# A bidirectional hybrid encoder layer: two small SBUF tiles that shift every pool's address, three score buffers in the attention, its output bank copied out at once, and a new order table

## The chip, the cores and the metric

One core of one Trainium2 chip runs the kernel. The metric is the device time in microseconds, as the median of several runs. The trace of one execution is read beside it.

## The reference, cut to what matters

The layer is FFN1, then a mixing stage of attention and RWKV-7 side by side, then FFN2; 1024 tokens, model width 1024, FFN width 2816, all in float32.

```
x = x + 0.5 * post1(FFN1(pre1(x)))          # SwiGLU: (silu(h @ w_gate) * (h @ w_up)) @ w_down
z = pre2(x) @ w_in                          # attention q|k|v and RWKV r|k|v|low-rank columns
attention: 8 heads of 64, rotary, three banded patterns (128,1), (512,4), (2048,16),
           mixed by their softmax denominators
RWKV-7:    8 heads, forward and backward delta-rule scans over the tokens, summed
x = x + post2(concat(attention, rwkv) @ w_out)
x = x + 0.5 * post3(FFN2(pre3(x)))
```

## The kernel before, in words

Large products are made from a rounded high part and a remainder: each operand is split into two `float32r` tiles, high (h) and low (l), and a product is three matmuls, h·h, h·l and l·h, of 128 rows by 128 stationary columns by up to 512 moving columns. The FFNs save one product in eight by Strassen's scheme, so a weight block meets seven sums of activation blocks (`_GateUp.multiply`, `down`). FFN1 takes the trace's first 620 us, FFN2 everything from about 1570 us on. Small products (scores of the far pattern, values, scan) are plain float32.

The attention works head by head. `far` handles the pattern of dilation 16, `near` the other two together, in eight query tiles t. For each t, `scores` makes up to 640 scores in PSUM, adds the bias and takes the minimum on DVE into the SBUF tile `sb`, and ACT takes the exponential there; `turn` transposes `sb` on PE and copies it to `e12`; `values` multiplies `e12` with v into the PSUM tile `po`, the one buffer of tag "o". When the last t is through, `near` weighs `po` by `c12` into the SBUF tile `ya`. `attention` loads the v tile of the far pattern, `v3`, into one buffer. The pool of all these tiles, `attw`, has two buffers for a tag that names no number.

Nothing is issued in the order in which it is written. `_Tape` records every operation with its tile accesses. `order` ranks them by a table of costs, going forward and backward over the graph, then adds to the rank of the operations with recorded numbers a to b what `LEADS` says, for one engine or all, and sweeps once more. The result is one fixed order per engine, which `play` issues. A buffer more or less, or another row of `LEADS`, can therefore move instructions anywhere between the FFNs.

SBUF is laid out by two stacks of pools. The left stack begins at byte 4224 of each partition with `cons` (the constants), and the right stack hangs from byte 229344 downwards. A tile takes its size rounded up to 32 bytes. `cons` holds, among others, two columns `eps0` and `eps1` and the column `root`, one float each and so 32 bytes each; `root` is written once by ACT and read by nobody.

Of the kernel before, what the change touches and what calls it, by code (L numbers as in the profile page):

```python
# [11 lines left out]
F32 = mybir.dt.float32  # L12
F32R = mybir.dt.float32r
AF = mybir.ActivationFunctionType
OP = mybir.AluOpType
# [5 lines left out]
NK, NT, NJ = D // 128, S // 128, DFF // 128  # L21
# [11 lines left out]
def _ap(src, off, pat):  # L33
    return bass.AP(tensor=src.tensor, offset=src.offset + off, ap=pat)


LEADS = (
# [6 lines left out]
)  # L44
LOADS = {AF.Exp: 1, AF.Sqrt: 2, AF.Silu: 3, AF.Tanh: 4}

# [682 lines left out]
class _Kernel:  # L729
# [537 lines left out]
    def near(self, psum, p, h, q1, q2, k, v, far, between):  # L1267

        nc, V, A, G, T = self.nc, self.nc.vector, self.nc.scalar, self.nc.gpsimd, self.nc.tensor
        hs = slice(h % 2 * 64, h % 2 * 64 + 64)  # L1270
        m, d, M, c12, c3 = (p.tile([128, NT], F32, name=n, tag=n) for n in ("m", "dn", "M", "c12", "c3"))
        po = psum.tile([128, NT, 64], F32, name="po", tag="o")
        S_, E_ = {}, {}
        keys = lambda t: (max(0, t - 2), min(NT, t + 3))

        def scores(t):
            k0, k1 = keys(t)
            n, qs = (k1 - k0) * 128, slice(t * 128, (t + 1) * 128)
            bias = self.bias12[:, (k0 - t + 2) * 128:(k0 - t + 2) * 128 + n]
            s = S_[t] = p.tile([128, 640], F32, name="sb", tag="sb")  # L1280
            for c in range(0, n, 512):
                e = min(n, c + 512)
                ps = psum.tile([128, 512], F32, name="s12", tag="w")
                T.matmul(ps[:, :e - c], q1[:, qs], k[:, k0 * 128 + c:k0 * 128 + e], start=True, stop=False)
                T.matmul(ps[:, :e - c], q2[:, qs], k[:, k0 * 128 + c:k0 * 128 + e], start=False, stop=True)
                V.tensor_tensor_reduce(out=s[:, c:e], in0=ps[:, :e - c], in1=bias[:, c:e], scale=1.0,
                                       scalar=m[:, t:t + 1] if c else 3e38, op0=OP.add, op1=OP.min,
                                       accum_out=m[:, t:t + 1])
            A.activation(s[:, :n], s[:, :n], AF.Exp, scale=-1.0, bias=m[:, t:t + 1], accum_out=d[:, t:t + 1])

        def turn(t):
            n, s = (keys(t)[1] - keys(t)[0]) * 128, S_.pop(t)
            et = E_[t] = p.tile([128, 640], F32, name="e12", tag="e12")
            for c in range(0, n, 512):
                w = min(n - c, 512)
                pt = psum.tile([128, 512], F32, name="pt12", tag="w")
                for i in range(w // 128):
                    T.transpose(pt[:, i * 128:(i + 1) * 128], s[:, c + i * 128:c + (i + 1) * 128], self.ident)
                A.copy(et[:, c:c + w], pt[:, :w])

        def values(t):
            (k0, k1), et = keys(t), E_.pop(t)
            for i in range(k1 - k0):
                for c in range(0, 128, 64):
                    T.matmul(po[c:c + 64, t, :], et[:, i * 128 + c:i * 128 + c + 64], v[:, k0 + i, hs], start=(i == 0),
                             stop=(i == k1 - k0 - 1))

        for step in range(NT + 2):
            if step < NT:
                between(step)  # L1310
                scores(step)
            if 1 <= step < NT + 1:
                turn(step - 1)
            if step >= 2:
                values(step - 2)
        f = far
        fm, fd = f[:, :, 64], f[:, :, 65]
        V.tensor_tensor(M, m, fm, op=OP.min)
        V.tensor_tensor(c12, m, M, op=OP.subtract)
        V.tensor_tensor(c3, fm, M, op=OP.subtract)  # L1320
        A.activation(c12, c12, AF.Exp, scale=-1.0)
        A.activation(c3, c3, AF.Exp, scale=-1.0)
        V.tensor_tensor(d, d, c12, op=OP.mult)
        V.tensor_tensor(M, fd, c3, op=OP.mult)
        V.tensor_tensor(d, d, M, op=OP.add)
        V.reciprocal(d, d)
        V.tensor_tensor(c12, c12, d, op=OP.mult)
        V.tensor_tensor(c3, c3, d, op=OP.mult)
        y = p.tile([128, NT, 64], F32, name="ya", tag="sb3", bufs=1)
        V.tensor_tensor(y, po, c12[:, :, None].to_broadcast([128, NT, 64]), op=OP.mult)  # L1330
        f3 = f[:, :, 0:64]
        G.tensor_tensor(f3, f3, c3[:, :, None].to_broadcast([128, NT, 64]), op=OP.mult)
        G.tensor_tensor(y, y, f3, op=OP.add)
        G.tensor_tensor(f3, y, y, op=OP.mult)
        V.tensor_reduce(out=self.ss_a[:, :, h], in_=f3, op=OP.add, axis=AX.X)
        self.nc.scalar.dma_start(_ap(self.ya_d, h * 64, [[512, 128], [128 * 512, NT], [1, 64]]), y)

    def attention(self, psum, p):
        X, F, ST = {}, {}, {}

        def load(pr):
            v3 = p.tile([128, 8, 128], F32, name="v3", tag="v3", bufs=1)
            for j in range(2):
                self.load(v3[j * 64:j * 64 + 64],
                          _ap(self.v_att, j * 512 + pr * 128, [[16 * 512, 64], [2 * 512, 8], [1, 128]]))
            vn = p.tile([128, NT, 128], F32, name="vn", tag="vn")
            self.load(vn, _ap(self.v_att, pr * 128, [[512, 128], [128 * 512, NT], [1, 128]]))
            q, k = (p.tile([128, S], F32, name=n, tag=n) for n in ("qp", "kp"))
            self.load(q, self.q_d[pr])
            self.load(k, self.kt_d[pr])  # L1350
            X[pr] = q, k, v3, vn

        def far(h):
            q, k, v3, _ = X[h // 2]
            for r in self.far(psum, p, h, q, k, v3):
                F[h] = r
                yield

        def stack(h):
            ST[h] = self.stacked(p, h)  # L1360

        load(0)
        for _ in far(0):
            pass
        stack(0)
        for h in range(H):
            nxt = far(h + 1) if h + 1 < H else iter(())

            def between(t):
                if t == 0 and h % 2 and h + 1 < H:  # L1370
                    load((h + 1) // 2)
                if t in (1, 3, 5):
                    next(nxt, None)
                if t == 4 and h + 1 < H:
                    stack(h + 1)

            self.near(psum, p, h, *ST.pop(h), X[h // 2][3], F.pop(h), between)
# [319 lines left out]
    def constants(self):  # L1697
        nc, io = self.nc, self.io
# [1 line left out]
        self.ident = cons.tile([128, 128], F32, name="ident")  # L1700
        make_identity(self.tc.nc, self.ident)
        self.g2c = self.column("mix_pre_g", NK)
        self.eps = {c: cons.tile([128, 1], F32, name=f"eps{i}") for i, c in enumerate((1.0, 0.5))}
        for c, t in self.eps.items():
            nc.vector.memset(t, EPS / (c * c))
        nc.scalar.activation(cons.tile([128, 1], F32, name="root"), self.eps[1.0], AF.Sqrt)
        self.gneps = cons.tile([128, 1], F32, name="gneps")
        nc.vector.memset(self.gneps, GN_EPS)
        self.h1_d, self.h2_d = self.dram("h1", [S, D]), self.dram("h2", [S, D])
# [53 lines left out]
    def run(self):  # L1763
        nc = self.nc
# [3 lines left out]
        natural = list(range(NT))  # L1768
        with self.top as top:

            self.constants()
            s_xn = ExitStack()
            xp = self.pool(s_xn, "xn")
# [3 lines left out]
            with ExitStack() as st:  # L1777
# [6 lines left out]
                f = self.factors(x, xt)  # L1784
# [31 lines left out]
                p = self.pool(s_f1, "ffn1")  # L1816
# [18 lines left out]
                y = [self.finish_low(rows, psum, ct, [ps[ct, half] for half in range(2)]) for ct in LO]  # L1835
# [4 lines left out]
                po = _Banks(w=pw, o=self.pool(s_ps, "ps_o", 1, space=PSUM))  # L1840
# [69 lines left out]
            for j in range(2):  # L1910
                for n in (1, 2):
                    gate_up.ready[n, j] = self.halves(wf, self.slab(wf, gate_up.source(j, 0, n - 1), bufs=2, queue=nc.gpsimd),
                                                      bufs=4)
            gb, late = self.row_bcast(hand, "mix_post_g"), {}
            f = self.factors(f0, None)
# [37 lines left out]
            with ExitStack() as st:  # L1953
# [13 lines left out]
                p, hand = self.pool(st, "ffn2", **R), self.pool(st, "hand3", **R)  # L1967
# [59 lines left out]
```

## Time and profile before

| | |
|---|---|
| median of 3 runs | 2223.08 us (2217.14 to 2230.62) |
| the profiled execution | 2219.22 us, of which the span from first to last instruction is 2217.4 us |
| busy: PE / DVE / ACT / POOL | 97% / 67% / 48% / 30% of the span |
| mean granted TensorE clock | 0.987 |
| matmul records | 14788 |

The span says how long the core worked; the profiled execution's own time has 1.8 us more around it. A busy engine is one that has an instruction in flight. Matmuls overlap: a 512-column matmul is in flight for about 395 ns, but the next one starts some 230 ns after it, so their rate is read from the starts, not from durations. [...]

### The profile page before, as it was taken

To read this page: it belongs to the slowest core of one execution; us is meant where nothing else is said; L and a number is where in the kernel's file an instruction comes from. 1 tells how busy PE (TensorE), PEld (TensorE's weight loads), DVE (VectorE), ACT (ScalarE), POOL (GpSimd) and SP (SyncE) were. 2 spreads that over 40 slices of the span, in tenths; PEclk is the share of its full clock that TensorE was granted. 3 is DMA by queue.
4 is the path that set the end of the run, shared out by engine and by line. 5 is a ranking of instruction groups with operands and counts; after the bars stand their busy time and mean duration, and the time that the engine had idled before them with its cause. 6 is when DMAs were issued, how large, how long until landed. Compare 5 with 4: busy or idle time off the path is not lost. (4 is left out here: it accounts for less than half of the span.)

```text
span 2217.4 us, 39926 instructions
## 1 busy us (share of the span) xinstructions
PE 2146.9 (97%) x14788; PEld 1738.5 (78%) x14788; DVE 1486.1 (67%) x2573; ACT 1064.0 (48%) x2026; POOL 662.4 (30%) x962
## 2 busy tenths in 40 slices
PE   6999999999999999999899998999899999999998
PEld 5888888878887888789687776767688888888887
DVE  8877767675575664663565557569976676776557
ACT  6333323354476655573666666456433323235453
POOL 3353444520000001142475661321053534451000
PEclk9999999999999999999899998999999999999999
DMA  5455444576463338776977757596254544458555
GB/s 152 133 166 162 158 161 138 180 272 213 152 233 121 122 135 278 209 233 205 264 219 194 178 138 179 128 283 204 85 182 139 176 141 149 138 198 308 187 179 185
DMA packets 364021, 403.36 MB, mean 182 GB/s; under 512 B 74418, under 2 KB 272306, under 8 KB 362804
## 3 DMA queue, kind: packets, MB, share of 16 engines
q1 hardware_dynamic: 319360, 309.47, 46.2%
q0 software_dynamic: 26416, 82.90, 11.0%
q10 hardware_dynamic: 18052, 8.46, 1.5%
q8 instruction: 116, 1.90, 0.4%
q14 instruction: 77, 0.63, 0.1%
HBM read 266.45 MB, written 134.28 MB: 181 GB/s over the span
## 5 line engine op out<-in xcount | busy, mean ns | idle before, releaser
L584 ACT ACTIVATE wh<-raw 128x512 fp32r<-128x512 f32 x264 | 163.7, 629 | 377.8 <-PE gu L584 304.4
L584 DVE TENSOR_TENSOR row<-gu,row 128x512 f32<-128x512 f32 x308 | 205.7, 686 | 193.3 <-PE gu L584 178.7
L584 POOL TENSOR_TENSOR row<-row 128x512 f32<-128x512 f32 x88 | 122.6, 1395 | 466.0 <-DVE row L584 448.5
L584 PE MATMUL gu<-xh,wh 128*128 128x512 f32 x704 | 253.9, 397 | 1.9 <-ACT row L584 1.6
L584 PE MATMUL gu<-xl,wh 128*128 128x512 f32 x704 | 253.6, 395 | 0.0
L584 PE MATMUL gu<-xh,wl 128*128 128x512 f32 x704 | 251.9, 395 | 0.0
L584 DVE TENSOR_TENSOR wl<-raw,wh 128x512 fp32r<-128x512 f32 x264 | 209.6, 813 | 18.1 <-ACT wh L584 14.4
L584 DVE TENSOR_TENSOR gwl<-graw,gwh 128x512 fp32r<-128x512 f32 (+2 forms) x187 | 115.8, 624 | 116.0 <-PE pd L584 85.5
L584 PE MATMUL pd<-gh,gwh 128*128 128x512 f32 x616 | 176.7, 395 | 0.4 <-ACT gh L584 0.4
L584 PE MATMUL pd<-gl,gwh 128*128 128x512 f32 x616 | 176.5, 395 | 0.0
L584 PE MATMUL pd<-gh,gwl 128*128 128x512 f32 x616 | 176.3, 395 | 0.0
L584 ACT ACTIVATE gwh<-graw 128x512 fp32r<-128x512 f32 (+2 forms) x187 | 102.8, 554 | 152.9 <-PE pd L584 119.2
L584 PEld LDWEIGHTS gu<-xh,wh 128*128 128x128 f32 x704 | 132.4, 189 | 33.0 <-ACT row L584 1.8
L584 PEld LDWEIGHTS gu<-xl,wh 128*128 128x128 f32 x704 | 132.2, 188 | 30.0
L584 PEld LDWEIGHTS gu<-xh,wl 128*128 128x128 f32 x704 | 131.9, 188 | 30.2
L584 PEld LDWEIGHTS pd<-gh,gwh 128*128 128x128 f32 x616 | 115.4, 188 | 27.5 <-ACT gh L584 0.8
L584 PEld LDWEIGHTS pd<-gh,gwl 128*128 128x128 f32 x616 | 115.5, 188 | 26.9
L584 PEld LDWEIGHTS pd<-gl,gwh 128*128 128x128 f32 x616 | 115.4, 188 | 27.0 <-DVE gl L584 0.5
L584 ACT ACTIVATE gh<-raw 128x512 fp32r<-128x512 f32 x160 | 99.4, 630 | 53.2 <-PE pd L584 31.0
L584 DVE TENSOR_TENSOR gl<-raw,gh 128x512 fp32r<-128x512 f32 x160 | 109.0, 694 | 20.7 <-ACT gh L584 20.7
L584 POOL TENSOR_TENSOR ws<-ws 128x512 f32<-128x512 f32 x88 | 118.0, 1340 | 2.9
L584 PE MATMUL zr<-xh,zh 128*128 128x512 f32 x320 | 107.0, 400 | 5.7 <-ACT zh L584 4.2
(298 smaller groups left out, 4817.6 us busy)
## 6 DMA issues: line engine op xcount, KB each, us to landing
d_hid<-row POOLq DMA_DIRECT2D x154, 256.0 KB, 3.0
graw<-d_hid SPq DMA_DIRECT2D x132, 256.0 KB, 3.0
raw<-in_ffn_w_up_dram SPq DMA_DIRECT2D x88, 256.0 KB, 3.2
ws<-in_ffn_w_down_dram SPq DMA_DIRECT2D x88, 256.0 KB, 4.3
d_ws<-ws POOLq DMA_DIRECT2D x88, 256.0 KB, 2.8
raw<-d_ws SPq DMA_DIRECT2D x88, 256.0 KB, 3.3
raw<-in_ffn_w_gate_dram SPq DMA_DIRECT2D x84, 256.0 KB, 3.2
raw<-in_ffn_w_down_dram SPq DMA_DIRECT2D x66, 256.0 KB, 3.3
```

The costliest lines, as they stand in the source:

```text
L584: i = getattr(getattr(self.nc, op.eng), op.method)(*op.args, **op.kwargs).ins
```

## The change

1. The column `root` moves into a second element of `eps0`, so `cons` is 32 bytes smaller and every pool of the left stack starts 32 bytes lower.
2. A tile `edge` of 120 floats (480 bytes) is put at the top of the right stack. Nothing reads or writes it; every pool of the right stack starts 480 bytes lower.
3. In `near`, `sb` and `e12` get three buffers; in `attention`, `v3` gets the pool's two.
4. `near` copies the PSUM tile `po` to `ya` on ACT, and DVE weighs `ya` in place; `ya` has a tag of its own and no longer shares the buffer of the far scores `sb3`.
5. The table `LEADS` has other rows. The costs and rules of the planner are as before.

```
-    (0, 1183, 8420, 0), (836, 1177, -1851), (1111, 1720, 1216), (2164, 2186, -51421, 1), (2215, 2730, 3599, 1),
...
+    (1213, 1316, 5853), (1562, 1602, 20982, 0), (1609, 1771, -10608, 0), (3774, 3934, 19691), (4092, 4123, 669, 0),
...
-            s = S_[t] = p.tile([128, 640], F32, name="sb", tag="sb")
+            s = S_[t] = p.tile([128, 640], F32, name="sb", tag="sb", bufs=3)
...
-            et = E_[t] = p.tile([128, 640], F32, name="e12", tag="e12")
+            et = E_[t] = p.tile([128, 640], F32, name="e12", tag="e12", bufs=3)
...
-        y = p.tile([128, NT, 64], F32, name="ya", tag="sb3", bufs=1)
-        V.tensor_tensor(y, po, c12[:, :, None].to_broadcast([128, NT, 64]), op=OP.mult)
+        y = p.tile([128, NT, 64], F32, name="ya", tag="ya", bufs=1)
+        A.copy(y, po)
+        V.tensor_tensor(y, y, c12[:, :, None].to_broadcast([128, NT, 64]), op=OP.mult)
...
-            v3 = p.tile([128, 8, 128], F32, name="v3", tag="v3", bufs=1)
+            v3 = p.tile([128, 8, 128], F32, name="v3", tag="v3")
...
-        self.eps = {c: cons.tile([128, 1], F32, name=f"eps{i}") for i, c in enumerate((1.0, 0.5))}
+        eps = [cons.tile([128, 2], F32, name=f"eps{i}") for i in range(2)]
+        self.eps = {c: t[:, :1] for c, t in zip((1.0, 0.5), eps)}
...
-        nc.scalar.activation(cons.tile([128, 1], F32, name="root"), self.eps[1.0], AF.Sqrt)
+        nc.scalar.activation(eps[0][:, 1:], self.eps[1.0], AF.Sqrt)
...
+            self.pool(top, "edge", side="right").tile([128, 120], F32, name="edge")
```

Where some pools start, in bytes of a partition, and the remainder on division by 128 (the operands of the large products lie a multiple of 512 bytes from their pool's start, but for 192 products of the low-rank and attention output kind):

| pool | what lies there | before | remainder | after | remainder |
|---|---|---|---|---|---|
| xn (left) | activations of FFN1 and of the projections (moving) | 7200 | 32 | 7168 | 0 |
| ffn1 (left) | moving operand of FFN1's down product | 72736 | 32 | 72704 | 0 |
| ring1 (right) | weight tiles of FFN1 (stationary) | 143328 | 96 | 142848 | 0 |
| zr (left) | weight tiles of the projections (stationary) | 72736 | 32 | 72704 | 0 |
| ring2 (left) | weight tiles of FFN2 (stationary) | 39968 | 32 | 39936 | 0 |
| xb0 (right) | activations of FFN2 (moving) | 196576 | 96 | 196096 | 0 |
| ffn2 (right) | moving operand of FFN2's down product | 118752 | 96 | 118272 | 0 |

Of the 7672 `float32r` matmuls, 2772 have moving and stationary remainders (32, 96), which is FFN1; 2772 have (96, 32), which is FFN2; 1872 have (32, 32), among them the projections; 256 have (96, 96). After, 7480 have (0, 0) and 192 have (64, 64). `attw` grows from 76800 to 88064 bytes and meets no pool that it did not meet before.

The order moves at these places. PE, where the attention's first head begins (`s` are scores, `q` and `kk` their operands, `pt<-ident,sb` the transposes of `turn`, `po<-vn,e` the values, `s<-kp,qp` far scores), before:

```order
L584 MATMUL s_2190<-kk,q_2180 128x384
L584 MATMUL s_2195<-kk,q_2180 128x512
L584 MATMUL s_2190<-kk,q_2181 128x384
L584 MATMUL s_2195<-kk,q_2181 128x512
L584 MATMUL pt_2197<-ident,sb 128x128 x3
L584 MATMUL s_2199<-kk,q_2180 128x512
L584 MATMUL s_2199<-kk,q_2181 128x512
L584 MATMUL s_2172<-kp,qp 64x64 x16
L584 MATMUL s_2200<-kk,q_2180 128x128
L584 MATMUL s_2200<-kk,q_2181 128x128
L584 MATMUL pt_2202<-ident,sb 128x128 x4
L584 MATMUL po<-vn,e_2196 64x64 x6
```

And the same place after:

```order
L584 MATMUL s_2193<-kk,q_2183 128x384
L584 MATMUL s_2198<-kk,q_2183 128x512
L584 MATMUL s_2202<-kk,q_2183 128x512
L584 MATMUL s_2203<-kk,q_2183 128x128
L584 MATMUL s_2193<-kk,q_2184 128x384
L584 MATMUL s_2198<-kk,q_2184 128x512
L584 MATMUL s_2202<-kk,q_2184 128x512
L584 MATMUL s_2203<-kk,q_2184 128x128
L584 MATMUL pt_2200<-ident,sb 128x128 x3
L584 MATMUL s_2209<-kk,q_2183 128x512
L584 MATMUL s_2209<-kk,q_2184 128x512
```

The scores of three query tiles now stand ahead of the first transposes, where two stood.

PE, at the end of the output projection, where FFN2's activations are transposed (`pt<-ident,row`) between its first products (`gu`), before:

```order
L584 MATMUL gu<-xh_3206,wh 128x512 x2
L584 MATMUL gu<-xl_3207,wh 128x512 x2
L584 MATMUL pt<-ident,row 128x128 x4
L584 MATMUL gu<-xh_3206,wl 128x512 x2
L584 MATMUL pt<-ident,row 128x128 x24
```

And after:

```order
L584 MATMUL gu<-xh_3209,wl 128x512 x3
L584 MATMUL pt<-ident,row 128x128 x16
L584 MATMUL gu<-xh_3209,wl 128x512
L584 MATMUL gu<-xh_3209,wh 128x512
L584 MATMUL gu<-xl_3210,wh 128x512
L584 MATMUL gu<-xh_3209,wl 128x512
L584 MATMUL gu<-xh_3209,wh 128x512
L584 MATMUL pt<-ident,row 128x128 x4
L584 MATMUL gu<-xl_3210,wh 128x512
L584 MATMUL gu<-xh_3209,wl 128x512
L584 MATMUL gu<-xh_3209,wh 128x512
L584 MATMUL gu<-xl_3210,wh 128x512
L584 MATMUL gu<-xh_3209,wl 128x512
L584 MATMUL pt<-ident,row 128x128 x8
```

Ten products that stood ahead of the run of 28 transposes now stand inside it. Over the whole PE queue the matmuls are the same in number and kind; changes from one shape of array tile to another (128x128, 128x64, 64x128, 64x64, 32x32) fall from 444 to 385.

## Rows read from the trace of the kernel before

**Rows 1.** The page, busy time of each engine.

```profile
PE 2146.9 (97%) x14788; PEld 1738.5 (78%) x14788; DVE 1486.1 (67%) x2573; ACT 1064.0 (48%) x2026; POOL 662.4 (30%) x962
```

**Rows 2.** Windows, PE alone: stretch, us, busy (matmuls touching it), clock, DMA share, GB/s.

```profile
100.00:400.00 300.00, 300.00 (x1312) 1.00 0.51 164
430.00:460.00 30.00, 30.00 (x130) 1.00 0.68 220
1600.00:1900.00 300.00, 300.00 (x1287) 1.00 0.49 160
```

**Rows 3.** Timeline of PE, projections: start us, us in flight, what, count.

```profile
964.82 0.39 PE L584 MATMUL zr<-xh,zh 128*128 128x512 f32 x1
...
969.80 0.62 PE L584 MATMUL zr<-xh,zl 128*128 128x512 f32 x2
```

**Rows 4.** Groups of PE instructions by shape: count, busy us, mean ns, idle before.

```profile
L584 PE MATMUL gu<-xh,wh 128*128 128x512 f32 x704 | 253.9, 397 | 1.9 <-ACT row L584 1.6 <-ACT wh L584 0.4
L584 PE MATMUL pd<-gh,gwh 128*128 128x512 f32 x616 | 176.7, 395 | 0.4 <-ACT gh L584 0.4
L584 PE MATMUL zr<-xh,zh 128*128 128x512 f32 x320 | 107.0, 400 | 5.7 <-ACT zh L584 4.2 <-DVE lm L584 0.9 <-ACT zy L584 0.4
L584 PE MATMUL gu<-t6l,wh 128*128 128x512 f32 x176 | 69.6, 396 | 0.0
```

**Rows 5.** Timeline of PE, two plain float32 passes beside output-projection products.

```profile
1493.82 1.02 PE L584 MATMUL yc<-f_y,k_cen 128*128 128x512 f32 x2
1494.27 0.79 PE L584 MATMUL op<-wol,xh 128*128 128x512 f32 x1
1494.90 0.39 PE L584 MATMUL op<-woh,xl 128*128 128x512 f32 x1
```

**Rows 6.** Timeline of PE in the attention: one transpose between values.

```profile
1079.14 1.12 PE L584 MATMUL po<-vn,e 128*64 128x64 f32 x16
1080.20 0.34 PE L584 MATMUL pt<-ident,sb 128*128 128x128 f32 x1
1080.46 0.69 PE L584 MATMUL po<-vn,e 128*64 128x64 f32 x16
```

**Rows 7.** Waits of PE, 1040 to 1340 us: for whom, us in total, times, longest.

```profile
PE po L584 <- ACT e L584: 2.1, 2, 1.3
PE s L584 <- DVE m L584: 2.0, 3, 0.8
PE pt L584 <- ACT sb L584: 1.9, 2, 1.5
PE pt L584 <- DVE m L584: 1.2, 4, 0.5
```

**Rows 8.** Timeline of PE at the end of the output projection.

```profile
1556.38 0.63 PE L584 MATMUL pt<-ident,row 128*128 128x128 f32 x4 [0.39 <-DVE row L584]
1558.84 0.63 PE L584 MATMUL pt<-ident,row 128*128 128x128 f32 x4 [1.84 <-DVE row L584]
1561.74 1.11 PE L584 MATMUL pt<-ident,row 128*128 128x128 f32 x4 [2.28 <-DVE row L584]
1564.84 1.09 PE L584 MATMUL pt<-ident,row 128*128 128x128 f32 x4 [1.98 <-DVE row L584]
1567.33 1.97 PE L584 MATMUL pt<-ident,row 128*128 128x128 f32 x8 [1.41 <-DVE xl L584]
```

**Rows 9.** Windows, all engines: us, PE, PEld, DVE, ACT, POOL busy, clock, DMA.

```profile
1050.00:1340.00 290.00, 272.57 (x4575) 222.50 (x4573) 167.08 (x434) 188.18 (x436) 179.49 (x383) 0.95 0.73 195
1556.00:1568.00 12.00, 4.12 (x19) 2.93 (x20) 11.91 (x21) 4.32 (x9) 0.00 (x0) 0.73 0.03 11
```

**Rows 10.** The tile ya: its users, ns shortest/median/longest, first and last start.

```profile
L584 DVE TENSOR_TENSOR ya<-po,c x8: 685/690/692, 1112.3 to 1337.0; 128x512 f32<-128x512 f32 x8
L584 POOL TENSOR_TENSOR ya<-ya,far x8: 1176/1184/1188, 1113.8 to 1338.5; 128x512 f32<-128x512 f32 x8
```

**Rows 11.** Groups of ACT instructions: the copies of transposed scores.

```profile
L584 ACT COPY e<-pt 128x512 f32<-128x512 f32 x56 | 32.5, 584 | 23.8 <-PE pt L584 23.1 <-POOL Ti L584 0.2
```

10 rows, old and new, of the table LEADS are left out of this document.

## The prediction

> **What bounds the kernel now.** I read the page first, then windows of PE over long steady stretches, then PE's timeline and waits between them. PE is busy 97% of the span and no other engine passes 67% [rows 1]; what shortens the run is fewer nanoseconds between the starts of PE's instructions. So the two numbers to look for are how far apart the starts of the large products lie, and where PE waits.
>
> The distance comes from a count. In 300 us of FFN1 there are 1312 matmuls, two of them cut by the edges: 300/1310 = 229.0 ns. In 300 us of FFN2 there are 1287: 300/1285 = 233.5 ns [rows 2]. In the projections 22 matmuls start between 964.82 and 969.80: 226.4 ns [rows 3]. [...] What differs is where the operands lie: FFN1 has remainders (32, 96) on 128 bytes, FFN2 (96, 32), the projections (32, 32). [...] One row speaks against addresses as the whole cause: from 430 to 460 us FFN1, with its usual addresses, also runs at 30/128 = 234 ns [rows 2].
>
> [...]
>
> **The change, part by part.** *Addresses (32 and 480 bytes).* All large products move to remainders (0, 0). The trace has no product there, so I bound the price. [...] At the worst, the products lock into the slow rhythm that the rows show, 233.5 ns. I take 226.4 ns, the best start distance that a row shows, in the projections, whose remainders are alike on both sides as the new ones are. FFN1 and FFN2 have 3696 `gu` and 1848 `pd` products (three kinds of 704 and nine of 176, three of 616) [rows 4], half in each FFN: 2772 each.
>
> - FFN1: 2772 x (229.0 - 226.4) = 7.2 us.
> - FFN2: 2772 x (233.5 - 226.4) = 19.7 us.
> - The projections and other products of that width stay at 226.4: 0.
>
> All of it lies on the path, since PE is busy for whole windows there [rows 2]. DVE, the next engine, has a third of its time free [rows 1]. DMAs start at new addresses as well, but cost the same per byte in FFN1 (0.51 of the engines for 164 GB/s) as in FFN2 (0.49 for 160), where the remainders are swapped [rows 2], and no large product waits for one: 0.
>
> *The order.* 59 fewer changes of array shape. [...] The ten products that now stand inside the run of transposes fill waits of 0.39 + 1.84 + 2.28 + 1.98 + 1.41 = 7.9 us [rows 8]; DVE is busy 11.91 of 12 us there [rows 9], so its chain ends when it ended, and what is gained is the ten products' own time: 2.3 us. If DVE's order delays that chain, the gain is lost, and PE waits for DVE again.
>
> *Third buffers for `sb` and `e12`.* They can remove PE's waits for ACT's exponential and copy and DVE's minimum: 2.1 + 2.0 + 1.9 + 1.2 = 7.2 us [rows 7]. Bounds 0 and 7.2; I take a third, 2.4, since a new order opens waits of its own between the same engines.
>
> *The copy of `po` and the rest.* Eight ACT copies of 584 ns [rows 11] are 4.7 us; ACT is busy 188 of 290 us in the attention [rows 9], so they lie beside other work: 0, and 4.7 if that cover goes. The DVE product keeps its 690 ns [rows 10], reading SBUF in place of PSUM. The bank comes free earlier, but no wait of PE in rows 7 is for that reader: 0. Behind the copy, on ACT's queue, wait exponentials of the next head, at most 0.6 us later. `v3` with two buffers, `root` and `edge`: no wait in the rows answers to them: 0.
>
> *The clock.* [...] The low stretches follow waits of PE, which the new order moves. Nothing says which way: 0, bounds 10 us on either side.
>
> Sum: 7.2 + 19.7 + 4.5 + 2.3 + 2.4 = 36.1 us off the profiled execution's 2219.2, which is 2183.1. The median of the runs stands 3.9 above that execution; on its footing it is 2187.0. I give the middle, **2185.0**.
>
> **The rivals.** [...]
>
> [...]
>
> *2. The addresses do nothing.* The stretch from 430 to 460 us [rows 2] shows the slow rhythm at FFN1's own addresses, so the distances may be two rhythms in which weight loads and columns fall, entered by chance. Then only 4.5 + 2.3 + 2.4 = 9.2 us come off: 2210, 0.4% faster.
>
> [...]
>
> *3. Slower: the slow rhythm everywhere.* Weights and columns now start on the same boundary in every product. If that makes the two fetches meet, FFN1 and the projections fall to FFN2's distance: 2772 x 4.5 = 12.5 and 1552 x 7.1 = 11.0 us more, less 9.2, so 2233.5. [...] For it: that rhythm holds for whole windows. Against it: the products with equal remainders are the quickest in the trace.
>
> **How the numbers follow.** The forecast's case, 2165 to 2205, has 0.38. Rival 1, from there down to 2090, has 0.25, since the half-rate passes are its only direct support. Rival 2, 2205 to 2220, has 0.24. Rival 3 has 0.13, with the clock's bad end in it. About 0.5%, 11 us, is what a measurement of this kernel can tell from no change. Faster by more: the first two cases and the edge of rival 2, 0.65; within: 0.22; slower: 0.13. The range reaches down into rival 1 to 2108 and up through rival 2 to 2226, leaving out some 0.09 at either end.
>
> **What the changed profile would show.** Windows of 300 us: over 1325 matmuls in both FFNs if the forecast holds; 1312 and 1287 again for rival 2; over 1360 for rival 1; 1287 in both for rival 3. The run of transposes near 1560 us should wait less than 6 us, and PE's waits for `e`, `m` and `sb` should sum to less than 7.2. I would be wrong if the FFN windows stand still and the time falls anyway, which would put the gain into the attention, or if the distances fall and DVE or DMA waits appear in the FFNs in their place.

## The result, and the profile after

The changed kernel takes 2189.74 us (median of 4 runs, 2187.66 to 2191.34) beside 2222.12 us for the kernel before in the same session: a ratio of 0.985, 95% interval 0.9818 to 0.9882. The profiled execution went from 2219.22 to 2187.66 us, 31.6 us less; the forecast was 2185.

The page of the changed kernel, busy time of each engine, to be held against [rows 1]:

```profile
span 2185.9 us, 39840 instructions
...
PE 2115.8 (97%) x14788; PEld 1736.2 (79%) x14788; DVE 1497.3 (68%) x2573; ACT 1064.1 (49%) x2034; POOL 671.2 (31%) x962
```

PE does the same 14788 matmuls and is as full as before. So the time went where the forecast looked for it, into the distance between starts. Windows of PE, the stretches of [rows 2]: us, busy (matmuls touching it), clock, DMA share, GB/s.

```profile
100.00:400.00 300.00, 299.50 (x1318) 1.00 0.50 165
430.00:460.00 30.00, 30.00 (x134) 1.00 0.65 212
1600.00:1900.00 300.00, 300.00 (x1325) 1.00 0.49 164
```

In FFN2, 1325 matmuls stand where 1287 stood: 300/1323 = 226.8 ns. In FFN1 it is 1318; the forecast had asked for over 1325 in both, so the mark is just missed. Seven starts there come 266 to 783 ns after the one before, which is 1.2 us more than their share and accounts for most of the missing products; the two longest hold the 0.5 us in which PE was idle. With the addresses alone and the old order (e1, below) there is one such start, and 1325 matmuls: the new order costs them. The stretch 430 to 460 us, slow before, now has 134. That cannot be put down to the addresses alone, since the kernel with the new order and the old addresses (e2, below) has 133 there.

Where the 31.5 us of the two profiled executions lie, from the ends of the products that close each stage (`gu` are the gate and up products of an FFN, `pd` its down products; FFN1's go on to 680.1 us in the kernel before, not to 620):

| stage | before, us | after, us | gained |
|---|---|---|---|
| to the last `pd` product of FFN1 | 680.1 | 674.9 | 5.2 |
| from there to the first `gu` product of FFN2 (projections, attention, scan, output projection) | 862.0 | 857.4 | 4.6 |
| the first 200 `gu` products of FFN2 and the transposes among them | 68.2 | 63.7 | 4.5 |
| from there to the last `pd` product | 599.9 | 582.7 | 17.2 |

### The profile page after: what moved, and what is told of

It reads as the page before. It is cut to its first block, busy times and chain, and to the rows that moved or that the text cites. A ratio compares the mean times of both kernels' runs of the same rounds, so it can differ in the third digit from the quotient of the medians.

```text
span 2185.9 us, 39840 instructions
## 1 busy us (share of the span) xinstructions
PE 2115.8 (97%) x14788; PEld 1736.2 (79%) x14788; DVE 1497.3 (68%) x2573; ACT 1064.1 (49%) x2034; POOL 671.2 (31%) x962
## 5 line engine op out<-in xcount | busy, mean ns | idle before, releaser
L584 DVE TENSOR_TENSOR wl<-raw,wh 128x512 fp32r<-128x512 f32 x264 | 222.6, 861 | 26.0 <-ACT wh L584 17.1
L584 PE MATMUL pd<-gh,gwh 128*128 128x512 f32 x616 | 181.9, 391 | 0.4 <-ACT gh L584 0.4
L584 PE MATMUL pd<-gh,gwl 128*128 128x512 f32 x616 | 181.9, 390 | 0.0
L584 PE MATMUL pd<-gl,gwh 128*128 128x512 f32 x616 | 181.4, 391 | 0.0
```

What stands on the lines that cost most here:

```text
L584: i = getattr(getattr(self.nc, op.eng), op.method)(*op.args, **op.kwargs).ins
```

## The experiments

Eleven kernels ran. "Remainder" is that of a pool's start on division by 512 from here on; on that footing the kernel before has 32 in the left stack and 480 in the right, and the changed kernel 0 and 0. Where no order is mentioned, PE's order is that of the kernel before, row for row. Kernels without an interval had one execution. The kernel before took from 2212.55 to 2234.34 us in twelve executions beside e9 to e11, so kernels with one execution are read by their windows, and their times are given beside.

**Addresses alone** (e1). The kernel before with the root column moved and the edge tile:

```
+        eps = [cons.tile([128, 2], F32, name=f"eps{i}") for i in range(2)]
+        self.eps = {c: t[:, :1] for c, t in zip((1.0, 0.5), eps)}
...
+        nc.scalar.activation(eps[0][:, 1:], self.eps[1.0], AF.Sqrt)
...
+            self.pool(top, "edge", side="right").tile([128, 120], F32, name="edge")
```

> The kernel before with the root column moved and the 480-byte edge tile, nothing else; PE's order is that of before. Theory 'addresses': the whole gain in the FFNs comes from where the operands start, so FFN1 takes 226.7 ns per product instead of 228.9 and FFN2 226.7 instead of 233.3; 2772 x 2.2 + 2772 x 6.6 = 24.4 us less, about 2198 us, windows of 300 us hold 1322 to 1326 matmuls in both FFNs, and the stretch 430 to 460 us holds 132 to 134. Rival 'order': the new order of work and the third buffers made PE's rhythm, the addresses nothing: about 2222 us, windows of 1312 and 1287 as before.

Measured: 2192.15 us, ratio 0.9866 (0.9839 to 0.9892). Its windows, columns as above:

```profile
100.00:400.00 300.00, 300.00 (x1325) 1.00 0.50 166
430.00:460.00 30.00, 29.61 (x131) 1.00 0.71 226
1600.00:1900.00 300.00, 300.00 (x1325) 1.00 0.48 159
```

1325 in both FFNs, with the old table, two buffers and no copy of `po`. The stretch 430 to 460 us has 131, with 0.39 us idle in it, where 132 to 134 were expected. The addresses alone bring 0.0134 x 2224.06 = 30 us (24 to 36), where 0.015 x 2222.12 = 33 us is the whole. The rival by which the order made PE's rhythm falls.

**The rest alone** (e2). The changed kernel without those lines; PE's order is that of the changed kernel:

```
+        self.eps = {c: cons.tile([128, 1], F32, name=f"eps{i}") for i, c in enumerate((1.0, 0.5))}
...
+        nc.scalar.activation(cons.tile([128, 1], F32, name="root"), self.eps[1.0], AF.Sqrt)
...
-            self.pool(top, "edge", side="right").tile([128, 120], F32, name="edge")
```

> The changed kernel without the moved root column and without the edge tile: new order, three buffers and the copy of po stay. Theory 'addresses': 24.4 us above the changed kernel's 2189.7, so about 2214 us, 8 us below the kernel before; windows of 1312 and 1287 in FFN1 and FFN2. Rival 'order': 2190 us, windows of 1318 to 1329.

Measured: 2222.21 us, ratio 0.9993 (0.9978 to 1.0007), from ten runs. Its windows:

```profile
100.00:400.00 300.00, 299.73 (x1308) 1.00 0.51 163
430.00:460.00 30.00, 30.00 (x133) 1.00 0.65 211
1600.00:1900.00 300.00, 300.00 (x1292) 1.00 0.48 156
```

Both FFNs are slow again. The stretch 430 to 460 us is not as slow as it was, though: at the same addresses the kernel before has 130 there and this one 133. In the kernel before, the distances in FFN1 go from 229, 226, 232 ns by turns to 233, 233, 234 at about 415 us and back at about 463, past a wait; here they stay at 229. So with unlike starts FFN1 can run in either of two rhythms at one pair of addresses, and what makes it enter the slower one stays open. The slow stretch cost the kernel before about 1 us.

New table, buffers, copy and `v3` come to 1.6 us together, between 4.9 gained and 1.6 lost; the 8 us that this expectation left to them are not there.

**One stack at a time** (e3, e4). First the root column alone (left 0, right 480), then the edge tile alone (left 32, right 0).

```
+        eps = [cons.tile([128, 2], F32, name=f"eps{i}") for i in range(2)]
...
+        nc.scalar.activation(eps[0][:, 1:], self.eps[1.0], AF.Sqrt)
```

> The kernel before with the root column moved alone: the left stack starts at remainder 0, the right stack stays at 96 (480 on division by 512). FFN1 has moving 0 and stationary 96, FFN2 moving 96 and stationary 0, the projections (0, 0). Theory 'alike' (a product is quick when both operands have the same remainder): both FFNs stay slow, 228 to 234 ns, windows of 1287 to 1314, total within 5 us of before. Theory 'round' (each operand that starts off a round address costs on its own): about half the gain in each FFN, 227.8 and 230.0 ns, windows of 1318 and 1305, total about 12 us below before.

```
+            self.pool(top, "edge", side="right").tile([128, 120], F32, name="edge")
```

> The kernel before with the 480-byte edge tile alone: the left stack stays at remainder 32 (on division by 512), the right goes to 0. FFN1 has moving 32 and stationary 0, FFN2 moving 0 and stationary 32. So far (0, 0) and (32, 32) are quick; pairs of 0 or 32 with 480 or 416 are slow, 229 to 233.3 ns, and the 64 products at (480, 480) lie at 230. Theory 'alike on 512 bytes' (both operands must have the same remainder on division by 512): slow here, 229 to 233 ns, windows of 1287 to 1312, about 2222 us. Theory 'late start' (an operand that starts 416 or 480 bytes into a block of 512 costs, one that starts at 0 or 32 does not): 226.7 ns in both FFNs, windows of 1322 to 1326, about 2198 us.

Measured: 2227.54 us (before: 2224.06) and 2226.15 us (before: 2226.62). Windows of the first:

```profile
100.00:400.00 300.00, 300.00 (x1288) 1.00 0.49 158
1600.00:1900.00 300.00, 300.00 (x1291) 1.00 0.47 156
```

and of the second:

```profile
100.00:400.00 300.00, 300.00 (x1287) 1.00 0.48 157
1600.00:1900.00 300.00, 300.00 (x1291) 1.00 0.48 156
```

(Where FFN2 begins late, a window from 1600 us on starts among the last transposes, which are short (0.109 us from one to the next in a row, the median in the kernel before) and add to the count: 8 of them in e2, e3, e4 and in e6 below, 16 in e5 below.)

Half of the change gains nothing; it even costs FFN1 its somewhat better 1312. A round start of one operand is worth nothing by itself, so "each odd operand costs on its own" falls, and with the second kernel so does "late start": 0 and 32, each harmless when both have it, are slow as a pair.

**Alike without being round.** Four kernels give the two stacks other starts. `pad` is an unread tile in the constants, which moves the left stack up. The first, e5, has 32 and 416:

```
+            self.pool(top, "edge", side="right").tile([128, 16], F32, name="edge")
```

> The kernel before with an edge tile of 64 bytes in place of 480 and no change to root: both stacks have remainder 32 on division by 128 (32 and 416 on division by 512), no operand starts on a round address. Theory 'alike': both FFNs run at 226.7 ns like the projections of before, windows of 1322 to 1326, about 2198 us. Theory 'round': nothing gained, windows of 1312 and 1287 or fewer, about 2222 us. If alike holds on 512 bytes and not on 128, the FFNs stay above 227.5 ns here.

The second, e6, has 32 and 32:

```
+            self.pool(top, "edge", side="right").tile([128, 112], F32, name="edge")
```

> The kernel before with an edge tile of 448 bytes and no change to root: both stacks have remainder 32 on division by 512, so every large product is at (32, 32), off any round address, like the projections of before. Theory 'alike on 512 bytes' and theory 'late start' both: 226.7 ns in the FFNs, windows of 1322 to 1326, about 2198 us. A theory by which only round addresses are quick in the FFNs, or by which what stands in the right stack matters: 229 ns or more, about 2222 us.

The third, e7, has 64 and 64:

```
+        cons.tile([128, 8], F32, name="pad")
...
+            self.pool(top, "edge", side="right").tile([128, 104], F32, name="edge")
```

> The kernel before with 32 bytes more in the constants and an edge tile of 416 bytes: both stacks have remainder 64 on division by 512. Theory 'alike on 512 bytes': 226.7 ns everywhere, about 2198 us. Theory 'late start': between the 32 that costs nothing and the 416 that costs 2 to 6 ns, so anything from 226.7 to 233 ns in both FFNs; it says that the projections move with the FFNs, since they now start at 64 too.

The fourth, e8, has 480 and 480:

```
+        cons.tile([128, 112], F32, name="pad")
```

> The kernel before with 448 bytes more in the constants: both stacks have remainder 480 on division by 512. Theory 'alike on 512 bytes': 226.7 ns in the FFNs and the projections, about 2198 us. Theory 'late start': both operands start late, FFNs at 230 to 234 ns and the projections slow as well, windows of 1285 to 1305; the projections alone would then lose 1000 to 1500 products x 3 to 6 ns = 3 to 9 us, so 2222 to 2240 us.

Measured: 2230.03 us for e5 (before: 2224.06), and 2206.6, 2194.74 and 2192.88 us for the others (before: 2226.62). FFN1 and FFN2 windows of e5, then of e6, e7 and e8:

```profile
100.00:400.00 300.00, 300.00 (x1292) 1.00 0.50 159
1600.00:1900.00 300.00, 300.00 (x1301) 1.00 0.47 153
```

```profile
100.00:400.00 300.00, 300.00 (x1325) 1.00 0.51 166
1600.00:1900.00 300.00, 300.00 (x1329) 1.00 0.50 162
```

```profile
100.00:400.00 300.00, 300.00 (x1325) 1.00 0.52 166
1600.00:1900.00 300.00, 300.00 (x1324) 1.00 0.49 159
```

```profile
100.00:400.00 300.00, 300.00 (x1325) 1.00 0.51 166
1600.00:1900.00 300.00, 300.00 (x1325) 1.00 0.49 158
```

Three alike pairs, (32, 32), (64, 64) and (480, 480), are as quick as (0, 0). (32, 416), alike on division by 128 and 32 but not by 256, is slow. Round addresses are not what makes these products quick. In e6 the FFN windows came out as expected, and the time did not: the middle of that execution was longer, of which more below.

**256 bytes apart** (e9). Root moved and an edge of 224 bytes: 0 and 256.

```
+            self.pool(top, "edge", side="right").tile([128, 56], F32, name="edge")
```

> The kernel before with the root column moved and an edge tile of 224 bytes: left stack at remainder 0, right stack at 256, on division by 512. Theory 'alike on 512 bytes': the operands of every FFN product are unlike, so 228 to 234 ns, windows of 1285 to 1312, about 2222 us. Theory 'alike on 256 bytes' (only the distance of the two starts on division by 256 counts): 226.7 ns in both FFNs, windows of 1322 to 1326, about 2198 us; 33 products of the output projection that already lie 256 apart in the changed kernel take mostly 226 and 227 ns, which speaks for it.

Measured: 2186.45 us (before: 2222.99). Its windows:

```profile
100.00:400.00 300.00, 300.00 (x1325) 1.00 0.51 166
1600.00:1900.00 300.00, 300.00 (x1325) 1.00 0.48 160
```

Alike on 256 bytes is enough, and e5 shows that alike on 128 is not. (The 33 products of the expectation are among FFN2's first, which stand between those of the output projection.)

**Third buffers alone** (e10), and the planner's order that follows from them:

```
-            s = S_[t] = p.tile([128, 640], F32, name="sb", tag="sb")
+            s = S_[t] = p.tile([128, 640], F32, name="sb", tag="sb", bufs=3)
...
-            et = E_[t] = p.tile([128, 640], F32, name="e12", tag="e12")
+            et = E_[t] = p.tile([128, 640], F32, name="e12", tag="e12", bufs=3)
```

> The kernel before with three buffers for the score tile sb and the exponential tile e12, nothing else; addresses in the FFNs, planner's costs and table as before, but the order of the attention moves with the buffers. The prediction gave this 2.4 us (bounds 0 and 7.2): then 2220 us, and PE's waits for e, m and sb between 1040 and 1340 us fall from 7.2 to 5 us or less. Rival 'order undoes it': the buffers move the order and open other waits, so 2223 us or more, with as much waiting in that stretch as before.

Measured: 2255.64 us, ratio 1.0147 (1.0118 to 1.0175). PE's waits for `e`, `m` and `sb` between 1040 and 1340 us, out of its view of waits (for whom, us in total, times, longest):

```profile
PE pt L584 <- DVE m L584: 2.3, 3, 1.3
PE s L584 <- ACT e L584: 0.9, 3, 0.4
PE pt L584 <- ACT sb L584: 0.9, 1, 0.9
PE pt L584 <- ACT e L584: 0.7, 1, 0.7
PE bp L584 <- DVE m L584: 0.7, 1, 0.7
PE po3t L584 <- ACT e L584: 0.7, 1, 0.7
PE po L584 <- ACT e L584: 0.6, 1, 0.6
```

They sum to 6.8 us, where [rows 7] have 7.2 (7.4 and 7.7 with the smaller ones): the buffers do not remove them. The whole middle of the run, from FFN1's last product to FFN2's first, as one window of PE:

```profile
682.50:1581.10 898.60, 836.89 (x9023) 0.95 0.64 183
```

beside the same stretch of the kernel before:

```profile
680.10:1542.10 862.00, 824.24 (x9018) 0.97 0.66 191
```

It is 36.6 us longer, 24 of them idle (61.7 beside 37.8), and the rest busy at a lower granted clock (0.95 beside 0.97). "Order undoes it" holds for this order; that every order would undo the buffers is not shown by one kernel.

**New table without the buffers** (e11). The changed kernel less the address lines and the third buffers:

```
-            s = S_[t] = p.tile([128, 640], F32, name="sb", tag="sb", bufs=3)
+            s = S_[t] = p.tile([128, 640], F32, name="sb", tag="sb")
...
-            self.pool(top, "edge", side="right").tile([128, 120], F32, name="edge")
```

> The changed kernel without the moved root column, the edge tile and the third buffers: the new table, the copy of po and the second v3 buffer stay. The whole of the new order with the buffers came to 0.9993 of before. If the buffers are worth 2 us or more of that, this is slower than before by 1 to 4 us (2224 to 2228 us); if the new table was made for three buffers, it is worse still, 2230 us or more; if the buffers do nothing, 2222 us as with them. In all of them the run of transposes at the end of the output projection keeps its products inside and its gain of 2 to 4 us, unless the table places them otherwise without the buffers.

Measured: 2238.59 us, ratio 1.0068 (1.0045 to 1.0092). The table is worse without the buffers, the buffers are worse without the table, and both together are at before. The gain at the transposes, which the expectation kept, is not there either: from FFN2's first product to its 200th this kernel takes 71.1 us, beside 68.2 before. The two parts cannot be priced apart: 1.0147 and 1.0068 would make 1.0216, and together they make 0.9993.

## Why the forecast held, step by step

The sum was 36.1 us against the profiled execution; it showed 31.5: 2.0 less than forecast in FFN1, 1.2 less in FFN2, 0.9 more at the transposes and 2.3 less in the middle. That this pair gained 4.6 us in the middle is in part luck: executions with one and the same order differ there by up to 17.6 us (below), and by e2 all that is not an address brings 1.6 us.

**The cause was named rightly, for half a reason.** The forecast took 226.4 ns since the projections' operands have alike remainders, "as the new ones are". e3 to e9 show that this was the point: like starts, not round ones. The prediction also said "remainders on 128 bytes". That was wrong: e5 is alike on 128 and slow, e9 is unlike on 512 and quick. The number is 256, as far as the differences tried here go. That the best distance of the old trace was the right one to take was known for half its reason, and so in part luck.

**FFN1, 7.2 us forecast.** 5.2 in the profiled execution. In the other kernels with alike starts FFN1 ended 3.5 to 7.1 us sooner than before (676.6 to 673.0 us), so the term is right and its size was at the upper end.

**FFN2, 19.7 us forecast.** 17.2 behind the first 200 products, and 16.9 there in each of e1 and e6 to e9. Two roundings make the difference: over all starts the mean was 233.3 ns before and 226.8 after, not 233.5 and 226.4, which is 2772 x 0.6 = 1.7; and the first 200 products, 1.3, are booked in the row of the table above it. That leaves 16.7.

**Ten products inside the run of transposes, 2.3 us forecast.** From FFN2's first product to its 200th it was 68.2 us before, 64.4 in the kernel with the rest alone, 66.6 with the addresses alone and 63.7 after. So the order gives some 3 to 4 us here, from single executions: those with the old order and alike starts (e1, e6 to e9) spread from 66.6 to 68.1. It is not the table's doing by itself, since e10, with the old table, takes 64.1 and e11, with the new one, 71.1. Timeline of PE in the changed kernel, to be held against [rows 8]:

```profile
1543.63 0.66 PE L584 MATMUL pt<-ident,row 128*128 128x128 f32 x4 [0.65 <-DVE row L584]
1545.59 1.23 PE L584 MATMUL pt<-ident,row 128*128 128x128 f32 x8 [1.30 <-DVE row L584]
1550.38 1.09 PE L584 MATMUL pt<-ident,row 128*128 128x128 f32 x4 [3.57 <-DVE row L584]
1551.12 0.78 PE L584 MATMUL gu<-xh,wl 128*128 128x512 f32 x1
...
1555.77 0.44 PE L584 MATMUL pt<-ident,row 128*128 128x128 f32 x2 [0.27 <-DVE xl L584]
```

The waits sum to 5.8 us where they were 7.9, under the forecast's mark of 6. DVE still sets the end of this chain (the third time of this window is its busy time, 14.00 of 14 us), as the step said:

```profile
1542.00:1556.00 14.00, 8.21 (x37) 5.96 (x36) 14.00 (x23) 6.06 (x11) 0.00 (x0) 0.76 0.33 125
```

**Fewer array-shape changes, 4.5 us, and third buffers, 2.4 us: the steps that failed.** With the transposes' 3 to 4 us, e2 (1.6 us in all, at most 4.9) leaves little or nothing for the two. No run shows the 4.5 us as a term of its own. The trace of the kernel before has 0.26 us from the start of the transpose of [rows 6] to the next start, at a mean granted clock of 0.89, and transposes of `turn` in a row start 0.109 us apart (the median of 208 at a clock of 1.00); if the other 0.15 us are two changes of shape, 59 fewer make 4.5 us, an estimate from one transpose. The middle shows how they were lost, set against the kernel with the addresses alone, which has none of them. First the changed kernel, then that one, as windows of PE from FFN1's last product to FFN2's first:

```profile
674.90:1532.30 857.40, 818.03 (x9017) 0.97 0.64 192
```

```profile
673.30:1529.90 856.60, 824.15 (x9019) 0.97 0.64 192
```

PE is busy for 6.1 us less and idle for 6.9 us more (39.4 beside 32.5). How long PE is busy also goes with its granted clock, which in the trace of the kernel before and in that of the changed kernel is either 1.00 or 0.50 (0.50 from 1060 to 1064 us of the kernel before). The same stretch of e2, which has the changed kernel's order:

```profile
679.70:1554.90 875.20, 824.06 (x9017) 0.96 0.65 188
```

Here no busy time is saved at first sight. But nine executions have the order of before (before, e1, e3 to e9), and their busy time in this stretch grows by about 0.375 us for each us that PE works at a granted clock of 0.50, to within 1.6 us. By that line, an estimate, 827.7 us were due for the changed kernel and 831.9 for e2; they have 818.0 and 824.1. So the new order does save PE 8 to 10 us of work, more than the 4.5 credited. Whether the changes of shape are the reason was not tried by itself; e10, with 391 of them, lies 3.8 us under the line, and e11, with 434, 1.1 over it. What the new order costs in return, 6.9 us of idle time and 3.0 of work at the lower clock, stood in the sum as 0.

The waits of the changed kernel between 1040 and 1340 us say what PE is idle for:

```profile
PE s L584 <- DVE lm L584: 3.2, 1, 3.2
PE pt L584 <- ACT e L584: 2.9, 3, 1.4
PE xu L584 <- ACT xs L584: 2.5, 2, 2.2
...
PE pa L584 <- DMA d<-d_t: 2.2, 2, 1.7
PE s L584 <- ACT e L584: 2.1, 5, 0.8
PE po L584 <- ACT e L584: 1.0, 2, 0.7
...
PE pt L584 <- DVE m L584: 0.7, 1, 0.7
...
PE pt L584 <- ACT sb L584: 0.4, 1, 0.4
```

Those for `e`, `m` and `sb` are 7.1 us (7.3 with the smaller ones, 7.7 before), which is [rows 7] over again, under other readers. It reads as if PE, running ahead by a third buffer, waited for the same engines at a later instruction; that was not tried by itself. Scan work (`lm`, `xs`, `d`) that another order had on time now comes late. The prediction had that mechanism ("a new order opens waits of its own") and still credited a third of the 7.2 us; by these waits it should have been 0. And what fewer shape changes save was credited in full, as if the new order left PE's idle time in the same stretch as it was.

**The copy of `po`, 0.** It is there at 586 ns each, and the product that follows keeps its duration (692 ns in the middle; the longest of the eight takes 1533). The tile `ya` of the changed kernel, to be held against [rows 10]:

```profile
L584 ACT COPY ya<-po x8: 565/586/592, 1105.8 to 1323.2; 128x512 f32<-128x512 f32 x8
L584 DVE TENSOR_TENSOR ya<-ya,c x8: 686/692/1533, 1132.5 to 1323.8; 128x512 f32<-128x512 f32 x8
```

It was not tried by itself; e2 bounds it only together with the rest.

**The clock, 0 within 10 us.** The middle has 0.97 before and after (its attention is in [rows 9]), but that is rounded: 44.4 us of it are at a granted clock of 0.50 before and 58.0 after, which by the line above costs some 4 us of busy time, inside the bound. The 10 us themselves are the author's estimate; no run shows them. That the low stretches come after waits of PE does show: leaving out the last 10 us of each trace, the kernel before has seven of them, and in the 12 us ahead of each PE is idle for 0.8 to 4.3 us, where the middle has 37.8 in 862; the changed kernel has eight, with 2.4 to 3.2 us ahead of each. The nine executions with the order of before took from 853.4 us (e9) to 871.0 (e6, with 71.7 us at the lower clock) for the middle. So a single execution cannot show a term of 2 to 5 us in the middle; FFN2 can, since it repeats to 0.3 us.

**The rivals.** Rival 1, with its mark of over 1360 matmuls in a window, falls: no window has over 1329, whatever the addresses. No run shows a distance that would give its 2090 us, or the 2108 at the foot of the range; the quickest steady one here is 226.7 ns. That plain float32 passes run at half the rate, on which its chance rested, is not shown either: by [rows 5] each takes about 0.425 us for 512 columns (1.08 us, less 0.23 for the product, for two), an estimate, beside 0.227 for a `float32r` product. The second (addresses do nothing) falls with e1. The row it stood on, 430 to 460 us, was read rightly: two rhythms at one pair of addresses do exist, but were seen with unlike starts alone, and the quicker of the two, 229, is still slower than 226.7. The third (weights and columns on the same boundary meet) has it the wrong way round: the same boundary is the quick case, 226.8 to 227.0 ns beside 229.0 to 233.3.

## What to carry to other kernels

Count matmuls in long full windows of each stage; if like instructions have unlike start distances, compare the start addresses of their stationary and moving operands before looking for waits. Here a few hundred unread bytes that made the two starts alike on division by 256 were worth 30 us of 2224, and moving one of the two alone was worth nothing. A third buffer in a program with a fixed, planned order is a new order first and a buffer second: price the waits that it opens as high as those that it closes, and set busy time against busy time only at like clocks.

## What the runs showed of the hardware

*The distance of two products goes here with the difference of two addresses.* Mean distance of consecutive starts of 128x128x512 `float32r` products, from the starts of all such matmul records 200 to 262 ns apart:

| stationary minus moving start, on division by 256 | where | ns |
|---|---|---|
| 0 | changed kernel, e1, e6 to e9, both FFNs | 226.8 to 227.0 |
| 32 or 224 | e3 and e4, both FFNs | 233.3 |
| 64 | before and e2, FFN2 | 233.3 |
| 192 | before (with its slow stretch), e2, FFN1 | 229.3, 229.0 |
| 128 | e5, FFN1 and FFN2 | 232.5, 232.8 |

Differences of 96 and 160 were not tried. e3 and e4 reach 32 and 224 from different absolute addresses and give the same mean. The projections, whose two operands lie in the same stack, have a median of 227 in every kernel here, e3 to e5 included; so it is the two operands of a product that count, and not how the stacks lie to each other. In the alike kernels the distances are a steady 227, 226, 227 ns, and no edit here went below that. In the slow stretch of the kernel before they are 233, 233, 234.

*In e4 it seems to be the weights of the next product that count.* There, 56 products with alike operands are followed by one whose weights lie in the other stack. The median distance from them to the next start is 231.5 ns for one direction and 234.5 for the other, beside 227 for the 1289 where the next weights are alike too. In e9, where the other stack is 256 away, 57 such places have 227. The loads that the profile lists do not get longer (means of 188 to 190 ns for the FFN products in before, after, e1, e3, e5, e7 and e9); why the start is put off stays open, and no edit here separates this from other readings.
